# Moving sums, squares and row products in a hybrid decoder layer, and adding the last part's weight blocks on VectorE

## The chip, the cores and the metric

The kernel runs on one core of a Trainium2 chip. The core has five engines with a queue each: TensorE (PE in the profile, its weight loads PEld) multiplies matrices into PSUM banks, VectorE (DVE) and ScalarE (ACT) work on elements, GpSimd (POOL) does small sums and issues transfers that add to what lies at their destination, and SyncE (SP) issues plain transfers. The metric is the device time of one execution in microseconds; of several runs the median counts.

## What is computed

One decoder layer on 512 tokens of width 1024, in float32. Cut to its outline, the reference is:

```python
x = x + 0.5 * swiglu(rms_norm(x, norm_ffn1_w), ffn1_w_in, ffn1_w_out)       # width 2816
x = x + hybrid_mixer(rms_norm(x, norm_mix_w), ...)     # SSD heads beside differential attention
x = x + memory_cross_attention(rms_norm(x, norm_cross_w), rms_norm(mem, norm_mem_w), ...)
x = x + 0.5 * swiglu(rms_norm(x, norm_ffn2_w), ffn2_w_in, ffn2_w_out)
return rms_norm(x, norm_final_w)
```

with

```python
def swiglu(h, w_in, w_out):
    gate, up = jnp.split(h @ w_in, 2, axis=-1)
    return (jax.nn.silu(gate) * up) @ w_out
```

The mixer's SSD half has 16 heads in four groups; each group's output is divided by the root mean square of its 256 columns. The attention half has 8 heads; both halves share an output projection.

## The kernel before

**Products in float32.** TensorE multiplies a rounded format (R32), so each operand is split: ScalarE writes the rounded value (`wh`, line 155) and VectorE the rest (`wl`, line 156), by `split_into`. A product is then three matmuls: high by high, high by low, low by high. Weights pass through a pool: six buffers `wr` for what a transfer brings, three `wh` and three `wl` for the split.

**Two by two blocks.** The big products of both FFNs are done with seven block products instead of eight. For that, sums of weight blocks are needed. Written with the four blocks B11, B12, B21, B22 of a weight, the output projection `out_blocks` uses B11, T1 = B12 + B11, T2 = T1 + B22, B21, B12 + B22, B22 and T4 = T2 + B21, each with its own combination of activation blocks (S1 to S4 and plain ones). Its products run in this order, each as 128x512 matmuls at line 1295: B11 and T1 turn by turn into `oa` and `oe`, T2 with S2 into `ob`, B21 into `oa`, B12 + B22 with S3 into `ob`, B22 with S4 into `oe`, T4 into `ob`. Between them, `oa` is copied into `ob` on ScalarE (line 1362), and `update` (line 1306) adds a finished bank to the running activations `x` on VectorE.

**Where the block sums come from.** In the second FFN they are made ahead of time in device memory (`isum`, `wsum`, by `block_sums_in_dram`). In the first FFN they are made on the way (`here` is true): T1 and B12 + B22 by a transfer from GpSimd that adds the second block to a buffer holding the first (`added`, line 1315), T2 by VectorE out of T1 and a fetched B22 (`t2`, line 1325), in the buffer of T1. T4 needs B21 added to the same buffer. In the first two parts, the fetched B21 is kept (`b21`, `later`) and added by VectorE after the B21 product (line 1372). In the last part `by_dma` is true: B21 is released after its split, and two adding transfers from GpSimd (`t4`, line 1336) read it again during the S3 product.

**Parts.** The 22 tiles of the FFN's inner width come in parts of 6, 8 and 8 (`THIRDS`); `out_blocks` runs once after each, and works on a part's weights in pieces of two tile pairs: in the second and third part, two pieces of 128x1024 a block. In the last part, the load of the memory tiles (`memory_in`) and a table (`prepare`) run beside it.

**Order.** `Order` traces the program. `dense` work is a list of generators that emit TensorE products; `chains` are small generators that yield a number of microseconds, after which they go on. Time in `Order` is the sum of the ideal times of the matmuls emitted. A dense generator that yields a function is blocked until that function is true. For SyncE's and GpSimd's queues the traced order is the order on the engine; on the other engines a planner orders the instructions when the program is built, by the traced order as priority and by when it expects their operands. `behind(ins)` holds what is traced in it behind the given instructions on their engine.

**Row products.** A column of 512 scale factors becomes a row, spread over 128 partitions, by `row_of`: two diagonal matrices (the rounded factors and the rest, line 376) are multiplied by ones into one bank `nrow`, two matmuls one behind the other. In `group` (the SSD groups) both diagonals are made on GpSimd.

**First output tile.** `out_attn` adds the attention half to `x`, four heads a call, eight output tiles. `load_w` fetches and splits a tile's weight. With `prep` all are loaded before the wait for the heads, else each in its turn.

**Squares.** Before the second FFN, `turn_last` transposes the last four tiles of `x`, and `row_of_last` squares them on ScalarE (line 556), 4.0 us later and 2.0 us apart. The first block product of that FFN (`quad` with `fresh`) is in flight then, with its copy of `qa` into `qb` at line 287.

Of the kernel before, what the change touches and what calls it, by code (L numbers as in the profile page):

```python
# [17 lines left out]
P = 128  # L18
# [9 lines left out]
THIRDS = ((0, 6), (6, 8), (14, 8))  # L28
# [9 lines left out]
W = {"h0": 3.4, "hs": 3.3, "ht": 2.0, "hv": 2.08, "hp": 6.75}  # L38
# [62 lines left out]
def body(tc, a, dbg=None):  # L101
# [13 lines left out]
    def nm(s):  # L115
        uid[0] += 1
        return f"{s}_{uid[0]}"

    def s2(s, dt=F32, shape=(P, T)):
        if math.prod(shape[1:]) <= T // 2:  # L120
            return sp.tile(list(shape), dt, tag="s1", name=nm(s), bufs=NHALF)
        return sp.tile(list(shape), dt, tag="s2", name=nm(s))

    def s4(s):
        return sp.tile([P, 4, T // 2], F32, tag=s, name=nm(s), bufs=1)

    def small(s, n, bufs=None):
        return tiny.tile([P, n], F32, tag=s, name=nm(s), bufs=bufs)
# [4 lines left out]
    def aux(s, shape=(P, T)):  # L133
        return aux_p.tile(list(shape), F32, tag="aux", name=nm(s))
# [5 lines left out]
    last, start, last_sum, recent, newest, newest_mm = [], [], [], [], [], []  # L140
    V, S, G = nc.vector, nc.scalar, nc.gpsimd
    od = Order()

    def mm(out, w, x, start, stop):
        od.t += (1 if w.dtype == R32 else 4) * (x.free_size() + 8) / 2400
        newest_mm[:] = [nc.tensor.matmul(out, w, x, start=start, stop=stop).ins]  # L146
# [5 lines left out]
    def split_into(hi, lo, src, scale=None):  # L152
        if scale is None:
            return (
                S.activation(hi, src, AF.Copy),  # L155
                V.tensor_tensor(lo, src, hi.bitcast(F32), ALU.subtract),  # L156
            )
        return (
            S.activation(hi, src, AF.Copy, scale=scale),
            V.scalar_tensor_tensor(lo, src, scale, hi.bitcast(F32), ALU.mult, ALU.subtract),  # L160
        )
# [10 lines left out]
    def load_w(src, n=D):  # L172
        raw = wp.tile([P, n], F32, tag="wr", name=nm("wr"), bufs=6)
        nc.sync.dma_start(raw, src)
        hi = wp.tile([P, n], R32, tag="wh", name=nm("wh"))
        lo = wp.tile([P, n], R32, tag="wl", name=nm("wl"))
        with ExitStack() as after:
            for i in start:
                after.enter_context(tc.issue_after(i))
            recent[:] = [i.ins for i in split_into(hi, lo, raw)]  # L180
        return hi, lo

    @contextmanager
    def behind(ins):
        with ExitStack() as after:
            for i in ins:
                after.enter_context(tc.issue_after(i))
            yield

    H = T // 2  # L190
    S1, S2, S3, S4 = "S1", "S2", "S3", "S4"
# [173 lines left out]
        G.tensor_tensor(col, v, mhalf[:, :nb], ALU.pow)  # L365
        return col

    def row_of(col, nb, first, second, apart):
        ch = tiny.tile([P, nb], R32, tag="ch", name=nm("ch"))
        first.tensor_copy(ch, col)  # L370
        cl = small("cl", nb)
        first.tensor_tensor(cl, col, ch.bitcast(F32), ALU.subtract)
        diags = []
        for eng, c in ((first, ch.bitcast(F32)), (second, cl)):
            diags.append(s2("ndiag", R32, (P, nb, P)))
            eng.tensor_tensor(diags[-1], ident[:, None, :].to_broadcast([P, nb, P]), c[:, :, None].to_broadcast([P, nb, P]), ALU.mult)
        yield apart
        pr = aux("nrow", (P, nb * P))
        with behind(list(newest_mm)):
            for j in range(2):  # L380
                mm(pr, ones_r, diags[j].rearrange("p a b -> p (a b)"), j == 0, j == 1)
        return pr

    class Stat:
# [109 lines left out]
    def ffn1(h, wa, at_out, each, done):  # L494
        xs = []
        wq, plain = iter(a["f1q"]), a["f1i"]
        col4, ncol4 = small("col4", 4, bufs=1), small("ncol4", 4, bufs=1)

        for ti, (_, nf) in enumerate(THIRDS):
            g = []  # L500
            nq = nf // 2
            made = block_tiles(g, nq, True)
            out = out_blocks(a[f"f1b{ti}"], None, g, col4, ncol4, each if ti == len(THIRDS) - 1 else None, n=nq, by_dma=ti == len(THIRDS) - 1)
            if ti == 0:
                th, f = s4("th"), 0
                for ps in ffn_first(h, wa):
                    if ps is None:
                        yield
                    else:
                        gated(*ps, st1.row, th, f)  # L510
                        f += 1
                made(th)
                V.tensor_scalar(col4, st1.col, 0.5, None, ALU.mult)
                V.tensor_scalar(ncol4, st1.col, -0.5, None, ALU.mult)
                for n in range(NPLAIN - 2):
                    for i in ((0, 1), (2,), (3,), ())[n]:
                        blocks = of_halves(h[2 * i], h[2 * i + 1])
                        b11 = tuple(s2("h11" + p_, R32, (P, H)) for p_ in "hl")
                        with behind(start):
                            for to, of in zip(b11, blocks["11"]):  # L520
                                S.activation(to, of.bitcast(F32), AF.Copy)
                        xs.append(block_sums(2 * i, C_FFN1, blocks | {"11": b11}, xf))
                    if n == 3:
                        xf.clear()
                    pg, pu = acc("pg"), acc("pu")
                    yield from proj(pg, load_w(plain[n][0]), h)
                    yield from proj(pu, load_w(plain[n][1]), h)
                    if n % 2 == 0:
                        th = s4("th")
                    if n == NPLAIN - 3:  # L530
                        next(out)
                    gated(pg, pu, st1.row, th, n % 2)
                    if n % 2:
                        made(th)
                h.clear()
                nq -= NPLAIN // 2
            yield from ffn_quads(xs, wq, st1, nq, made, BY_BLOCK, prime=out)
            at_out(ti)
            if ti == len(THIRDS) - 1:
                xs.clear()  # L540
            yield from out
        done()
        banks = [acc, aux, acc, aux]
        yield from turn(1, banks)
        yield from turn(0, banks)
# [303 lines left out]
    wcv = []  # L849

    def out_attn(hg, o0, o1, prep=False):
        ws = {o: load_w(a["woa"][hg, o], 4 * P) for o in range(o0, o1) if prep}
        yield lambda: all(y is not None for y in ya[4 * hg : 4 * hg + 4])
        heads = ya[4 * hg : 4 * hg + 4]
        for o in range(o0, o1):
            po = acc("pm")
            yield from proj(po, ws.get(o) or load_w(a["woa"][hg, o], 4 * P), heads)
            V.tensor_tensor(x[o], x[o], po, ALU.add)
            if prep and len(wcv) < 2:
                wcv.append(load_w(a["wcv"][len(wcv)]))  # L860
        if o1 == KT:
            ya[4 * hg : 4 * hg + 4] = [None] * 4
# [44 lines left out]
    def group(g, bt, ct, xs, zs):  # L907
# [97 lines left out]

        rh = inv_rms_cols(pn, 4, 4.0 / (4 * 256), 4.0 * EPS)
        yield W["gn"]
        pr = yield from row_of(rh, 4, G, G, W["gr"])
        for j in range(2):
            n = 2 * g + j  # L1010
            V.scalar_tensor_tensor(yz[j], yz[j], par[:, C_SSD + n : C_SSD + n + 1], pr, ALU.mult, ALU.mult)
# [252 lines left out]
    def out_blocks(blocks, sums, g, col4, ncol4, each=None, finale=None, clean=True, n=None, by_dma=False):  # L1264

        early = n is not None
        n = n or len(g)
        parts = [(k, min(k + 2, n)) for k in range(0, n, 2)]
# [29 lines left out]
        def product(ps, of, which, first=False, ready=None):  # L1298
            for part in parts:
                w = ready if ready and part == parts[0] else weights(of, part)  # L1300
                for t in range(2):
                    yield from some(ps[t], w, which, part, t, first)
# [36 lines left out]
        here = sums is None  # L1339
        if here:  # L1340
            sums = [t1, added(blocks[B12], blocks[B22], "gate"), t2, lambda part: t_raw[part]]
# [7 lines left out]
        b_ps = [bank[t]("ob") for t in range(2)]  # L1349
# [8 lines left out]
        for m in both:  # L1358
            yield from m
        u2 = []  # L1360
        for t in range(2):
            S.activation(b_ps[t], a_ps[t], AF.Copy)
        for t in range(2):
            update(t + 2, 1, e_ps[t], 1, False)
        yield from product(b_ps, sums[2], S2)
        for t in range(2):
            u2.append(s2("u2"))
            S.activation(u2[t], b_ps[t], AF.Copy)
# [94 lines left out]

    def turn_last():
        yield from turn(1)
        od.spawn(row_of_last(), 4.0)

    def row_of_last():
        for k in range(4, KT):
            with behind(list(newest)):  # L1470
                squared(k, x[k])
            yield 2.0
        yield from row_from(st_2, 3.0)

    od.add(turn_last())
# [90 lines left out]
```

## Time and profile before

| | us |
|---|---|
| runs | 1309.28, 1312.72, 1312.79 |
| median of the runs | 1312.72 |
| the profiled execution, its own time | 1310.71 |
| its span in the profile | 1308.9 |

| engine | busy us | share of the span |
|---|---|---|
| PE | 1288.9 | 98% |
| DVE | 971.9 | 74% |
| ACT | 706.5 | 54% |
| POOL | 119.5 | 9% |

The span runs from the first to the last instruction of the program. Timeline rows have the start in us from there, the duration, engine, line of the kernel, operation, `out<-in` by tile names, shapes and a count; a bracket at the end tells how long the engine sat idle before and what released it. Rows of the same kind that follow each other are merged into one with a count. Rows of waits have who waited for whom, then the total in us, the times and the longest. Matmuls overlap, so the step from one start to the next, and not the duration, is what a matmul costs.

### The profile page before, as it was taken

Reading aid. Unit: us, or ns where it says so; the run is one execution under the profiler, and the core shown is the slowest. Engines: PE = TensorE matmul, PEld = TensorE weight load, DVE = VectorE, ACT = ScalarE, POOL = GpSimd, SP = SyncE. Lnnn points to the kernel's source line nnn. Section 1 sums busy time; section 2 is a strip of 40 time slices with the busy share of each in tenths; the row PEclk is TensorE's granted clock in tenths of the full one; section 3 lists DMA queues with packets and bytes.
Section 4 is the critical chain, followed back from the end, with each engine's and each line's share of the span. In section 5 each row is a group of like instructions: output and inputs, shape, how many; then the busy total and the mean of one; then the engine's idle time right before and its main releaser. Section 6 shows DMA issues by size and latency. Waiting matters only on the chain.

```text
span 1308.9 us, 20080 instructions
## 1 busy us (share of the span) xinstructions
PE 1288.9 (98%) x7709; PEld 1123.8 (86%) x7709; DVE 971.9 (74%) x1542; ACT 706.5 (54%) x1208; POOL 119.5 (9%) x149
## 2 busy tenths in 40 slices
PE   9999999999999999999999999999999999999997
PEld 7879988997887778777788878888889999989995
DVE  6977888787875676567867687645677878877886
ACT  7545564565754564346645465434365646555564
POOL 0001010001110011101012021020001000000000
PEclk9999999999999999999999999999999999999999
DMA  9367777777974525663475638684248876666662
GB/s 339 88 174 187 196 198 196 217 201 203 292 239 146 137 65 148 226 165 105 94 202 156 193 124 240 192 215 131 65 122 249 212 234 179 188 194 180 182 204 96
DMA packets 69263, 234.75 MB, mean 179 GB/s; under 512 B 8160, under 2 KB 9664, under 8 KB 68816
## 3 DMA queue, kind: packets, MB, share of 16 engines
q1 hardware_dynamic: 53200, 180.91, 41.5%
q0 software_dynamic: 13168, 45.67, 19.5%
q10 hardware_dynamic: 2800, 6.91, 1.6%
q8 instruction: 60, 0.98, 0.3%
q14 instruction: 35, 0.29, 0.1%
HBM read 231.30 MB, written 48.29 MB: 214 GB/s over the span
## 4 chain that ended last, share of the span: by engine, by line
PE 75%; issue 13%; DVE 4%; DMA 3%; ACT 2%; POOL 1%; POOLq 0%; SPq 0%; ACTq 0%; DVEq 0%
PE qb L243 11%; PE pm L146 10%; PE qa L243 8%; PE qe L243 7%; PE ob L1295 5%; PE pxbc L146 4%; PE pcq L146 3%; PE pz L146 3%; PE oa L1295 3%; PE oe L1295 3%; DMA wr<-in_f1b 2%; PE pa L146 2%; PE pcv L146 2%; PE pg L146 2%; PE pu L146 2%
## 5 line engine op out<-in xcount | busy, mean ns | idle before, releaser
L155 ACT ACTIVATE wh<-wr 128x1024 fp32r<-128x1024 f32 (+1 forms) x323 | 328.3, 1018 | 339.8 <-issue 60.4
L156 DVE TENSOR_TENSOR wl<-wr,wh 128x1024 fp32r<-128x1024 f32 (+1 forms) x323 | 378.1, 1175 | 138.6 <-ACT wh L155 135.9
L772 ACT ACTIVATE ec<-ec,mn 128x512 f32<-128x512 f32 (+3 forms) x64 | 35.3, 554 | 33.7 <-DVE mn L771 33.7
L146 PE MATMUL pxbc<-hnh,wh 128*128 128x512 f32 x128 | 52.6, 411 | 0.0
L146 PE MATMUL pxbc<-hnh,wl 128*128 128x512 f32 x128 | 50.2, 392 | 0.0
L146 PE MATMUL pxbc<-hnl,wh 128*128 128x512 f32 x128 | 50.2, 392 | 0.0
L243 PE MATMUL qb<-s24h,wh 128*128 128x256 f32 x152 | 43.1, 284 | 0.8 <-ACT qb L287 0.8
L243 PE MATMUL qa<-hmh,wl 128*128 128x256 f32 x152 | 43.1, 284 | 0.1
L243 PE MATMUL qe<-s24h,wl 128*128 128x256 f32 x152 | 43.1, 284 | 0.0
L243 PE MATMUL qa<-h11h,wh 128*128 128x256 f32 x152 | 43.1, 283 | 0.0
L243 PE MATMUL qb<-s24h,wl 128*128 128x256 f32 x152 | 43.0, 283 | 0.0
L243 PE MATMUL qa<-h11h,wl 128*128 128x256 f32 x152 | 43.0, 283 | 0.0
L243 PE MATMUL qb<-s31h,wh 128*128 128x256 f32 x152 | 43.0, 283 | 0.0
L243 PE MATMUL qb<-s31l,wh 128*128 128x256 f32 x152 | 43.0, 283 | 0.0
L243 PE MATMUL qb<-s31h,wl 128*128 128x256 f32 x152 | 43.0, 283 | 0.0
L243 PE MATMUL qa<-hml,wh 128*128 128x256 f32 x152 | 43.0, 283 | 0.0
L243 PE MATMUL qe<-s24h,wh 128*128 128x256 f32 x152 | 43.0, 283 | 0.0
L243 PE MATMUL qa<-h11l,wh 128*128 128x256 f32 x152 | 43.0, 283 | 0.0
L243 PE MATMUL qa<-hmh,wh 128*128 128x256 f32 x152 | 43.0, 283 | 0.0
L243 PE MATMUL qe<-s24l,wh 128*128 128x256 f32 x152 | 43.0, 283 | 0.0
L243 PE MATMUL qb<-hml,wh 128*128 128x256 f32 x152 | 43.0, 283 | 0.0
L243 PE MATMUL qb<-hmh,wh 128*128 128x256 f32 x152 | 43.0, 283 | 0.0
(457 smaller groups left out, 4170.1 us busy)
## 6 DMA issues: line engine op xcount, KB each, us to landing
wr<-in_f2q SPq DMA_DIRECT2D x44, 512.0 KB, 4.5
wr<-in_f1q SPq DMA_DIRECT2D x40, 512.0 KB, 4.5
wr<-in_f1b SPq DMA_DIRECT2D x25, 512.0 KB, 6.6
isum<-in_f2q SPq DMA_DIRECT2D x22, 512.0 KB, 5.2
wr<-isum SPq DMA_DIRECT2D x22, 512.0 KB, 4.1
wsum<-in_f2b SPq DMA_DIRECT2D x20, 512.0 KB, 5.6
wr<-wsum SPq DMA_DIRECT2D x20, 512.0 KB, 4.7
wr<-in_f1q POOLq DMA_DIRECT2D x16, 512.0 KB, 6.8
```

The costliest lines, as they stand in the source:

```text
L146: newest_mm[:] = [nc.tensor.matmul(out, w, x, start=start, stop=stop).ins]
L155: S.activation(hi, src, AF.Copy),
L156: V.tensor_tensor(lo, src, hi.bitcast(F32), ALU.subtract),
L243: newest_mm[:] = [nc.tensor.matmul(out, a_[:, wc], b_, start=first and f == 0 and kp == 0 and j == 0, stop=kp == n - 1 and j == 2, skip_gr ...
L772: S.activation(ec[:, :n], ec[:, :n], AF.Exp, bias=mn, scale=-1.0, accum_out=sm[c][:, i : i + 1])
L1295: newest_mm[:] = [nc.tensor.matmul(ps, a_[:, ts], b_[:, ws], start=first and k == 0 and j == 0, stop=k == n - 1 and j == 2, skip_group_che ...
```

## The change

Five edits. `row_of` gets a parameter `between`: what a chain yields between the two row products; the SSD groups pass 1.2 us, all others nothing. The call of `out_blocks` in the first FFN no longer passes `by_dma`, so the last part too keeps B21 and adds it on VectorE. `out_attn` loads the weight of output tile 0 before it asks for the heads. In `out_blocks`, all sums T2 are traced before the copies and updates ahead of the S2 product, rather than piece by piece within it; only the first FFN does this. `row_of_last` starts at 6.5 us with 1.2 us between squares.

```diff
-    def row_of(col, nb, first, second, apart):
+    def row_of(col, nb, first, second, apart, between=()):
...
-        with behind(list(newest_mm)):
-            for j in range(2):
+        for j in range(2):
+            with behind(list(newest_mm)):
                 mm(pr, ones_r, diags[j].rearrange("p a b -> p (a b)"), j == 0, j == 1)
+            if j == 0:
+                yield from between
         return pr
...
-            out = out_blocks(a[f"f1b{ti}"], None, g, col4, ncol4, each if ti == len(THIRDS) - 1 else None, n=nq, by_dma=ti == len(THIRDS) - 1)
+            out = out_blocks(a[f"f1b{ti}"], None, g, col4, ncol4, each if ti == len(THIRDS) - 1 else None, n=nq)
...
-        ws = {o: load_w(a["woa"][hg, o], 4 * P) for o in range(o0, o1) if prep}
+        ws = {o: load_w(a["woa"][hg, o], 4 * P) for o in range(o0, o1) if prep or o == 0}
         yield lambda: all(y is not None for y in ya[4 * hg : 4 * hg + 4])
...
-        pr = yield from row_of(rh, 4, G, G, W["gr"])
+        pr = yield from row_of(rh, 4, G, G, W["gr"], (1.2,))
...
         u2 = []
+        second = {part: t2(part) for part in parts} if here else {}
         for t in range(2):
             S.activation(b_ps[t], a_ps[t], AF.Copy)
         for t in range(2):
             update(t + 2, 1, e_ps[t], 1, False)
-        yield from product(b_ps, sums[2], S2)
+        yield from product(b_ps, second.get if here else sums[2], S2)
...
-        od.spawn(row_of_last(), 4.0)
+        od.spawn(row_of_last(), 6.5)
...
                 squared(k, x[k])
-            yield 2.0
+            yield 1.2
         yield from row_from(st_2, 3.0)
```

## The prediction

> **What bounds the kernel now.** I read the page first, for the share of each engine.
>
> ```profile
> span 1308.9 us, 20080 instructions
> ...
> PE 1288.9 (98%) x7709; PEld 1123.8 (86%) x7709; DVE 971.9 (74%) x1542; ACT 706.5 (54%) x1208; POOL 119.5 (9%) x149
> ```
>
> TensorE is busy nearly all the time, and no matmul is added or removed. The edit can therefore win only what TensorE now waits for, and lose only by new waits. So I read the waits of TensorE next (total us, times, longest).
>
> ```profile
> PE ob L1295 <- DVE wl L156: 1.7, 3, 0.8
> ...
> PE ob L1295 <- ACT wh L155: 1.1, 1, 1.1
> ...
> PE qb L243 <- ACT qb L287: 0.8, 1, 0.8
> ...
> PE nrow L146 <- POOL ndiag L376: 0.5, 1, 0.5
> ```
>
> These rows are small: 4.1 us together, 0.31% of the span. Then I found each of them in the timelines. The largest cluster is in the last part of the first FFN's output projection, in its product S2 and then in S3:
>
> ```profile
> 316.41 0.39 PE L1295 MATMUL ob<-wh,s24h 128*128 128x512 f32 x1
> ...
> 317.44 0.50 PE L1295 MATMUL ob<-wl,s24h 128*128 128x512 f32 x1 [0.41 <-DVE wl L156]
> ...
> 321.12 0.50 PE L1295 MATMUL ob<-wh,s24h 128*128 128x512 f32 x1 [1.11 <-ACT wh L155]
> ...
> 324.35 0.39 PE L1295 MATMUL oa<-wh,gh 128*128 128x512 f32 x1
> ...
> 332.90 0.40 PE L1295 MATMUL ob<-wh,s31l 128*128 128x512 f32 x1
> 333.82 0.50 PE L1295 MATMUL ob<-wl,s31h 128*128 128x512 f32 x1 [0.53 <-DVE wl L156]
> ```
>
> What S2 takes without waits is shown by the same 24 matmuls of the part before, a piece of the chain of waits:
>
> ```profile
> 195.73 5.44 PE ob L1295 x24
> ```
>
> That is 0.23 us from one to the next. Here S2 takes 324.35 - 316.41 = 7.94 us, so 2.5 are lost. In S3 the step from 332.90 to 333.82 is 0.92 instead of 0.23: 0.7 lost.
>
> **The change, part by part.**
>
> *Sums of the S2 weight pieces made earlier.* VectorE's and ScalarE's rows around it:
>
> ```profile
> 313.17 1.22 DVE L1325 TENSOR_TENSOR wr<-wr,wr 128x1024 f32<-128x1024 f32 x1
> ...
> 314.90 0.75 DVE L1306 SCALAR_TENSOR_TENSOR x<-oe,col,x 128x512 f32<-128x512 f32 x1
> ...
> 316.17 1.23 DVE L156 TENSOR_TENSOR wl<-wr,wh 128x1024 fp32r<-128x1024 f32 x1
> ...
> 318.75 1.23 DVE L1325 TENSOR_TENSOR wr<-wr,wr 128x1024 f32<-128x1024 f32 x1
> 321.10 1.22 DVE L156 TENSOR_TENSOR wl<-wr,wh 128x1024 fp32r<-128x1024 f32 x1 [1.12 <-ACT wh L155]
> ```
> ```profile
> 320.01 1.06 ACT L155 ACTIVATE wh<-wr 128x1024 fp32r<-128x1024 f32 x1 [3.14 <-DVE wr L1325]
> ```
>
> The second sum runs at 318.75, behind two running-sum updates (L1306) of which one is shown; ScalarE's split waits 3.14 us for it, TensorE 1.11 us for the split. Now both sums stand ahead of the copies and updates, so the second can run after the first. No sum is added here, one of 1.23 us is moved ahead, and what is queued behind it is the low split of the first piece (316.17), which already ended (317.40) too late for TensorE. In the bad order that split is 1.2 us later: the 0.4 us wait grows to 1.6 and S2 wins only 2.5 - 1.6 = 0.9, with the second split then in time. In the good order (the sum in a hole of VectorE before 316) it wins 2.5. In the part before, S2 has nothing to win (its 5.44 above), and the third wait of ob on wl (0.8 of the 1.7 us) lies in S3 of the first part, whose sums stay: I take 0 for both. SyncE's fetches keep their order, five of this projection one after another with nothing of another line between them, so no queue is passed:
>
> ```profile
> 298.59 16.15 SPq L1276 DMA_DIRECT2D wr<-in_f1b  x5
> ...
> 320.00 0.33 SPq L1276 DMA_DIRECT2D wr<-in_f1b  x1
> 323.88 5.96 SPq L174 DMA_DIRECT2D wr<-in_wck  x3
> ```
>
> The fetch at 320.00 leaves when the second sum (318.75 + 1.23 = 319.98) gives its buffer back, so it will leave 2 to 4 us sooner.
>
> *The last running sums by VectorE.* Two adding transfers on GpSimd's queue (L1336) go; block 21, fetched anyway, stays in its two buffers and is added by two more VectorE sums (2 x 1.22 = 2.44 us) after the 12 product's splits. Is there room? Busy us in two stretches: PE, PEld, DVE, ACT, POOL; then clock, DMA share and GB/s.
>
> ```profile
> 316.00:324.40 8.40, 6.82 (x28) 4.64 (x27) 7.28 (x10) 4.83 (x8) 2.54 (x5) 1.00 0.94 242
> 324.40:336.00 11.60, 11.07 (x48) 8.62 (x47) 8.33 (x13) 6.89 (x14) 1.70 (x3) 1.00 1.05 276
> ```
> ```profile
> 324.90 0.69 DVE L1369 TENSOR_TENSOR oe<-oe,u 128x512 f32<-128x512 f32 x1
> 328.26 1.22 DVE L156 TENSOR_TENSOR wl<-wr,wh 128x1024 fp32r<-128x1024 f32 x1 [2.66 <-ACT wh L155]
> ...
> 332.54 1.23 DVE L156 TENSOR_TENSOR wl<-gate,wh 128x1024 fp32r<-128x1024 f32 x1 [0.61 <-ACT wh L155]
> ```
>
> VectorE is free for 11.60 - 8.33 = 3.27 us of the second stretch, 2.66 of them in one hole ending at 328.26. The sums fit into that hole: cost 0; without it, up to 2.44. They hold the buffers longer: the wck fetches of 323.88, next in SyncE's queue, wait for them until 324.90 + 0.69 + 1.22 = 326.8 and 328. Their first user starts far behind:
>
> ```profile
> 350.54 0.48 PE L146 MATMUL pck<-hm,wh 128*128 128x256 f32 x2
> ```
>
> So this costs nothing. What S3 waits for is something else, the landing of its own two adding transfers:
>
> ```profile
> 327.17 1.06 ACT L155 ACTIVATE wh<-wr 128x1024 fp32r<-128x1024 f32 x1 [2.94 <-DMA wr<-in_f1b]
> ...
> 331.45 1.06 ACT L155 ACTIVATE wh<-gate 128x1024 fp32r<-128x1024 f32 x1 [1.55 <-DMA gate<-in_f1b]
> ```
>
> The second piece lands at 331.4, its low split ends at 332.54 + 1.23 = 333.77, and TensorE uses it at 333.82: no slack. If that landing stays, everything that S2 wins is waited for again in S3, and the two edits together win 0. If it comes earlier by d, they win d, at most 2.5 + 0.7 = 3.2. The DMA engines are full there (share 0.94 and 1.05), and the change takes two adding transfers of 512 KB and for some 3 us two fetches out of that stretch. Bounds 0 and 3.2; I take 1.4, just under the middle, since the first piece (327.17) leaves S3 only some 0.9 us of room by itself: its low split ends at 328.26 + 1.22 = 329.48, and its first use is 11 matmuls ahead of the one at 332.90, at about 330.4.
>
> *The row products of the SSD groups* are parted by 1.2 us of other matmuls.
>
> ```profile
> 780.42 0.49 PE L146 MATMUL nrow<-ndiag,ones_r 128*128 128x512 f32 x1
> 781.42 0.49 PE L146 MATMUL nrow<-ndiag,ones_r 128*128 128x512 f32 x1 [0.50 <-POOL ndiag L376]
> ...
> 815.67 0.62 PE L146 MATMUL nrow<-ndiag,ones_r 128*128 128x512 f32 x2
> ```
> ```profile
> 780.34 1.03 POOL L376 TENSOR_TENSOR ndiag<-ident,cl 128x512 fp32r<-128x512 f32 x1
> ```
>
> In group 2 the second product comes 1.00 us after the first instead of 0.23, since GpSimd's diagonal ends at 781.37. With 1.2 us between it is ready: 0.77 won. In the last group the two run together (815.67). There the order is blocked until the group is done, so no matmul falls between them: 0; were it held back, the first output projection would wait up to 1.2. The group's scaling comes 1.2 us later elsewhere, long before its use. I take 0.8 won.
>
> *The first output tile's load* is traced before the wait for the heads, not after.
>
> ```profile
> 502.29 0.60 PE L150 MATMUL pot<-ident,on 128*128 128x128 f32 x4
> ...
> 511.04 0.40 PE L146 MATMUL pm<-yah,wh 128*128 128x512 f32 x1
> ```
>
> The last head's transposes (502.29) precede the first output matmul (511.04) by 8.7 us and it shows no wait: the condition holds when it is asked, and nothing moves. 0.
>
> *The squares before the second FFN* start 2.5 us later and stand closer.
>
> ```profile
> 976.07 1.06 ACT L155 ACTIVATE wh<-wr 128x1024 fp32r<-128x1024 f32 x1 [0.25 <-PE qa L243]
> 977.03 0.58 ACT L287 ACTIVATE qb<-qa 128x512 f32<-128x512 f32 x1
> ```
>
> The copy that TensorE waits 0.8 us for stands behind a weight split, and that split had waited 0.25 us for TensorE, with ScalarE idle: the square ahead of it was done by then. Moving the square frees nothing unless it also changes who goes first. Bounds 0 and 0.8; I take 0.3, a third of it.
>
> **Sum.** 1.4 + 0.8 + 0.3 = 2.5 us. The profiled run took 1310.71 us (span 1308.9 and 1.8 around it), so 1308.2 against it; the runs' median, 1312.72, lies 2.0 higher, so 1310.2.
>
> **Rivals.**
> - *All of it comes back.* S2 2.5, S3 0.7, the row product 0.8, the copy 0.8: 4.8, so 1307.9. For it: each edit stands at a place with a wait. Against: it needs the S3 transfers over 3 us sooner.
> - *The adding transfers were hidden anyway.* They were issued after those S3 needs. Landing times of the two removed, then of all twelve that stay in the first FFN (min, median, max):
>
> ```profile
> DMA to landing us min/median/max: 11.9/13.5/15.2
> ...
> DMA to landing us min/median/max: 4.3/8.1/9.6
> ```
>
>  The removed ones took 13.5 us against 8.1, as if they stood behind the others rather than beside them. Then S3's landings stay, part three wins 0, and only 0.8 + 0.3 is left: 1311.6. [...]
> - *VectorE becomes the bound of part three (slower).* The moved sum delays the first low split by 1.2 and the two new sums stand ahead of S3's splits instead of in the hole: 1.2 + 2.44 = 3.7 and nothing won, 1316.4, more if the wck fetches wait as well. It decides when the new sums start after 327. For it: VectorE is busy 7.28 of 8.40 us in S2. Against: the hole of 2.66 us, right behind the splits that the sums follow.
>
> **How the numbers follow.** Forecast 1310.2 (its own range 1308.9 to 1311.6): 0.40. All back: 0.22. Hidden anyway: 0.13. Slower: 0.25. A change under 0.3% (3.9 us, the spread of the three runs) can't be told from none. Faster than 1308.8 is the second case and a quarter of the first: 0.32. Slower than 1316.7 is two thirds of the last: 0.17. The rest, 0.51, is the same. The range 1307.0 to 1315.8 leaves out the edge of the second case and part of the last.
>
> **What would show it.** Right: the wait on ACT wh near 321 gone, both L1325 sums together near 314, two L1372 sums before 329, the gate piece's split starting near 330, no nrow wait on POOL. Wrong: L1372 behind L1306 at 331; the S3 wait grown to 2 us with the same landing (hidden anyway); a wait at pck; new waits of 1 us in the SSD groups, whose hand order shifts by 1.2 us.

## The result and the profile after

| | us |
|---|---|
| before, median of 7 runs beside the change | 1310.82 (1308.98 to 1312.79) |
| after, median of 7 runs | 1316.65 (1314.33 to 1317.26) |
| ratio, with its 95% interval | 1.0038 [1.0025, 1.005] |
| the profiled execution after, its own time and span | 1317.26 and 1315.5 |

The change makes the kernel 0.38% slower, 5.8 us. The forecast was 2.5 us faster (1310.2, reckoned from 1312.72, the median of the first three runs). In the code of after the lines stand 2 or 3 lower: L1295 is now L1297, L1325 is L1327, L1372 is L1375, L1011 is L1013.

TensorE's waits after (who waited for whom; total us, times, longest), the rows that answer to those of before:

```profile
PE ob L1297 <- DVE wl L156: 4.7, 3, 2.1
PE pq L146 <- DVE vl L156: 3.1, 1, 3.1
...
PE qb L243 <- ACT qb L287: 0.8, 1, 0.8
...
PE nrow L146 <- POOL ndiag L376: 0.5, 1, 0.5
```

The second row is new. The wait of `ob` on `wh` (1.1) is gone, and that on `wl` has grown from 1.7 to 4.7. The waits that the row products and the squares were to end, `nrow` and `qb`, are what they were. The two stretches that lost most follow.

**SSD group 0, near 560 us.** The profiled execution after is 2.08 us behind that of before at the first row product (560.59 against 558.51), 5.09 us at the first matmul of `pq` (567.71 against 562.62) and 6.68 us at the 14th (572.38 against 565.70): 4.6 us are lost here. TensorE's timeline after, and then before:

```profile
560.59 0.39 PE L146 MATMUL nrow<-ndiag,ones_r 128*128 128x512 f32 x1
...
562.20 0.39 PE L146 MATMUL nrow<-ndiag,ones_r 128*128 128x512 f32 x1
...
567.71 0.50 PE L146 MATMUL pq<-hnh,wh 128*128 128x512 f32 x1 [3.06 <-DVE vl L156]
...
568.98 0.63 PE L146 MATMUL pq<-hnh,wl 128*128 128x512 f32 x1
...
572.38 0.39 PE L146 MATMUL pq<-hnl,wh 128*128 128x512 f32 x1
```
```profile
558.51 0.62 PE L146 MATMUL nrow<-ndiag,ones_r 128*128 128x512 f32 x2
...
562.62 0.50 PE L146 MATMUL pq<-hnh,wh 128*128 128x512 f32 x1
...
565.70 0.39 PE L146 MATMUL pq<-hnl,wh 128*128 128x512 f32 x1
```

The second row product comes 1.61 us after the first; six matmuls of the value projection `pv` lie between them. The query projection `pq`, which started without a wait before, waits 3.06 us. VectorE after, and before:

```profile
562.63 1.41 DVE L1013 SCALAR_TENSOR_TENSOR y<-y,par,nrow 128x512 f32<-128x512 f32 x2 [1.57 <-PE nrow L146]
564.08 1.35 DVE L156 TENSOR_TENSOR ysl<-y,ysh 128x512 fp32r<-128x512 f32 x2
565.83 1.22 DVE L156 TENSOR_TENSOR wl<-wr,wh 128x1024 fp32r<-128x1024 f32 x1 [0.40 <-ACT wh L155]
566.97 2.48 DVE L156 TENSOR_TENSOR vl<-pv,vh 128x512 fp32r<-128x512 f32 x4
```
```profile
559.17 1.41 DVE L1011 SCALAR_TENSOR_TENSOR y<-y,par,nrow 128x512 f32<-128x512 f32 x2 [0.18 <-PE nrow L146]
560.62 1.35 DVE L156 TENSOR_TENSOR ysl<-y,ysh 128x512 fp32r<-128x512 f32 x2
561.89 1.28 DVE L156 TENSOR_TENSOR vl<-pv,vh 128x512 fp32r<-128x512 f32 x2
563.75 1.23 DVE L156 TENSOR_TENSOR wl<-wr,wh 128x1024 fp32r<-128x1024 f32 x1 [0.58 <-ACT wh L155]
```

ScalarE after:

```profile
563.42 1.29 ACT L155 ACTIVATE ysh<-y 128x512 fp32r<-128x512 f32 x2 [3.61 <-DVE y L1013]
564.74 1.06 ACT L155 ACTIVATE wh<-wr 128x1024 fp32r<-128x1024 f32 x1
...
565.71 2.04 ACT L155 ACTIVATE vh<-pv 128x512 fp32r<-128x512 f32 x4
```

The scaling of `y` waits for the second row product, with VectorE idle for 1.57 us. Behind it stand the two splits of `y`, and behind these the splits of `pv` into `vh` and `vl`. These free the four accumulation banks that `pv` holds, and `pq` needs one of them. Before, the first of the two `vl` of 561.89 (0.68 of the 1.28 us) ended at 562.57, 0.05 us ahead of `pq`. After, a weight split (`wh`, `wl`) that had stood behind the first two `v` splits stands ahead of all four. So `vl` starts at 566.97.

Behind the wait, the matmuls step 0.43 us apart (568.98 to 572.38 are eight steps) instead of 0.23. The stretches after, with the busy us of PE, PEld, DVE, ACT, POOL, then TensorE's granted clock, DMA share and GB/s, and one of before:

```profile
564.00:568.00 4.00, 0.94 (x4) 0.48 (x4) 3.56 (x6) 3.68 (x7) 0.81 (x1) 1.00 0.99 256
568.00:572.00 4.00, 4.00 (x13) 3.09 (x13) 1.45 (x3) 0.00 (x0) 0.00 (x0) 0.62 0.97 303
572.00:576.00 4.00, 4.00 (x18) 3.30 (x17) 0.00 (x0) 1.08 (x2) 0.00 (x0) 0.96 0.04 18
```
```profile
562.00:566.00 4.00, 3.94 (x18) 2.95 (x17) 3.42 (x5) 2.25 (x4) 0.81 (x1) 1.00 0.91 245
```

The granted clock falls to 0.62 in the 4 us from 568 on, and read finer it is 0.97 from 568 to 569, 0.50 from 569 to 572 and 0.82 from 572 to 573. Eight steps, 0.2 us longer each, are 1.6 us; with the 3.0 us by which `pq` starts later, they make the 4.6 us.

**The last part of the first FFN.** TensorE in S2, and at S3:

```profile
317.54 0.40 PE L1297 MATMUL ob<-wh,s24h 128*128 128x512 f32 x1
...
320.76 0.50 PE L1297 MATMUL ob<-wl,s24h 128*128 128x512 f32 x1 [2.14 <-DVE wl L156]
...
325.43 0.39 PE L1297 MATMUL oa<-wh,gh 128*128 128x512 f32 x1
...
333.17 0.50 PE L1297 MATMUL ob<-wl,s31h 128*128 128x512 f32 x1 [1.69 <-DVE wl L156]
```

S2 takes 325.43 - 317.54 = 7.89 us, where it took 7.94. Its waits of 0.41 and 1.11 have become one of 2.14; with S3's they have grown by 1.8 us (2.14 + 1.69 - 0.41 - 1.11 - 0.53). VectorE, ScalarE and GpSimd:

```profile
314.30 1.22 DVE L1327 TENSOR_TENSOR wr<-wr,wr 128x1024 f32<-128x1024 f32 x1
...
316.04 1.22 DVE L1327 TENSOR_TENSOR wr<-wr,wr 128x1024 f32<-128x1024 f32 x1
...
319.49 1.22 DVE L156 TENSOR_TENSOR wl<-wr,wh 128x1024 fp32r<-128x1024 f32 x1
...
325.52 2.35 DVE L1375 TENSOR_TENSOR wr<-wr,wr 128x1024 f32<-128x1024 f32 x2
330.50 0.70 DVE L1372 TENSOR_TENSOR oe<-oe,u 128x512 f32<-128x512 f32 x1 [2.62 <-ACT u L1371]
...
331.89 1.22 DVE L156 TENSOR_TENSOR wl<-wr,wh 128x1024 fp32r<-128x1024 f32 x1
```
```profile
328.92 1.06 ACT L155 ACTIVATE wh<-wr 128x1024 fp32r<-128x1024 f32 x1 [4.05 <-DMA wr<-in_f1b]
...
331.70 1.06 ACT L155 ACTIVATE wh<-gate 128x1024 fp32r<-128x1024 f32 x1
```
```profile
320.75 0.87 POOL L1317 DMA_DIRECT2D wr<-in_f1b  x1 [17.90 <-DVE wl L156]
```

Both T2 sums now stand ahead of the first piece's low split (319.49), which S2 waits for. The two sums that replace the adding transfers run at 325.52, in VectorE's hole. S3's first weight piece lands later than before (its split at 328.92, against 327.17), since GpSimd's issue of it waits until that same low split is done (320.71); from issue to landing it takes 8.1 us, as before (8.2). The second piece's split starts about when it did (331.70, against 331.45).

S3's wait of 1.69 us is for the first piece's low split, and by these rows the order on VectorE makes it (no run tests that alone). ScalarE's split of that piece is done at 329.98 (328.92 + 1.06), but VectorE's starts only at 331.89: it stands behind an update of `oe` (330.50) that waits for ScalarE's copy `u`, which ScalarE makes after its split. Started at 329.98, it would have ended at 331.20 by its 1.22 us, just ahead of its use (due at 331.09 + 0.23, one step behind the matmul before it). Before, it stood ahead of that update, at 328.26:

```profile
329.40 0.69 DVE L1369 TENSOR_TENSOR oe<-oe,u 128x512 f32<-128x512 f32 x1
```

### The profile page after: what moved, and what is told of

Same layout as the page of the kernel before. It is cut to its first block, busy times and chain, and to the rows that moved or that the text cites. A ratio compares the mean times of both kernels' runs of the same rounds, so it can differ in the third digit from the quotient of the medians.

```text
span 1315.5 us, 20076 instructions
## 1 busy us (share of the span) xinstructions
PE 1289.9 (98%) x7709; PEld 1124.6 (85%) x7709; DVE 974.3 (74%) x1544; ACT 707.4 (54%) x1208; POOL 118.6 (9%) x147
## 4 chain that ended last, share of the span: by engine, by line
PE 75%; issue 13%; DMA 4%; DVE 4%; ACT 2%; POOL 1%; POOLq 0%; SPq 0%; ACTq 0%; DVEq 0%
PE qb L243 11%; PE pm L146 10%; PE qa L243 7%; PE qe L243 7%; PE ob L1297 5%; PE pxbc L146 4%; PE oa L1297 3%; PE pcq L146 3%; PE oe L1297 3%; PE pz L146 3%; DMA wr<-in_f1b 2%; PE pa L146 2%; PE pcv L146 2%; PE pq L146 2%; PE pg L146 2%
## 5 line engine op out<-in xcount | busy, mean ns | idle before, releaser
L243 PE MATMUL qb<-hmh,wl 128*128 128x256 f32 x152 | 43.0, 283 | 0.0
```

The costliest lines, as they stand in the source:

```text
L243: newest_mm[:] = [nc.tensor.matmul(out, a_[:, wc], b_, start=first and f == 0 and kp == 0 and j == 0, stop=kp == n - 1 and j == 2, skip_gr ...
```

## The experiments

Every ratio is to the kernel before on the same chip, with its 95% interval.

### Which of the edits

All edits but the parted row products:

```diff
-        pr = yield from row_of(rh, 4, G, G, W["gr"], (1.2,))
+        pr = yield from row_of(rh, 4, G, G, W["gr"])
```

> All five edits but the 1.2 us between the row products. Theory: the parted row product of SSD group 0 holds VectorE's queue, so the value splits and with them the banks of the next projection come late (3.06 us of wait, then some 1.6 us of slow clock). Then this kernel shows no wait of pq on vl, full clock there, and takes about 4.8 us less than the changed kernel: some 1312 us against 1310.8 before (ratio about 1.001). Rival: the wait at pq comes from the shift of the work ahead (part three of the first FFN is 1.7 us later). Then it stays and the time is about 1316.5 (1.004).

Measured: 1311.34 us, ratio 1.0007 [0.9994, 1.0019]; no wait at `pq`. In the last part of the first FFN its profiled execution waits 1.67 and 1.01 us where after shows 2.14 and 1.69.

The parted row products alone, with `between` of `row_of` and the call above as in the change, and nothing else:

> The kernel before with the 1.2 us between the row products alone. Theory: the wait of pq on vl of about 3 us and the slow clock behind it are there, time about 1315.6 (ratio 1.0037). Rival (they come from the sums ahead): no such wait, time as before, 1310.8. In both the wait of nrow on GpSimd in group 2 stays at 0.5 us, since its two products stay adjacent in the order.

Measured: 1316.03 us, ratio 1.0046 [1.0028, 1.0063]. The wait of 3.06 us stands at `pq`, with slow steps behind it (0.42 to 0.43 us from 565.42 on, a granted clock of 0.66 from 566 to 570); the wait of 0.50 us in group 2 is still there. So this edit alone makes the whole slowdown, and the other four together nothing that can be told from none.

### Which group

The parting in group 0 alone, then in all others:

```diff
-        pr = yield from row_of(rh, 4, G, G, W["gr"])
+        pr = yield from row_of(rh, 4, G, G, W["gr"], (1.2,) if g == 0 else ())
```
```diff
-        pr = yield from row_of(rh, 4, G, G, W["gr"])
+        pr = yield from row_of(rh, 4, G, G, W["gr"], (1.2,) if g else ())
```

> The kernel before with the two row products parted by 1.2 us in the first SSD group alone. Theory (the slowdown is made in the first group: the scaling comes some 1.4 us late, the weight's split then goes ahead of two splits of v, the q projection waits 3.1 us and its next eight products run at half clock): about 1315.9, the whole of what the parting in all groups showed (1316.0 against 1310.8 in those runs), with the wait of 3.1 us and the slow steps in the trace. Rival (the groups behind it bring part of it): 1312 to 1314.

> The kernel before with the products parted by 1.2 us in the second, third and last group, adjacent in the first. Theory: 1310.8, no change; the 0.5 us wait of the third group stays, since the planner sets six products ahead of the first row product there instead of between the two. Rival: 1312 to 1314, with a wait in one of these groups that was not there.

Measured: 1314.17 us, 1.0038 [1.0022, 1.0054], for group 0; 1310.82 us, 1.001 [1.0, 1.0019], for the others (before: 1309.85). Group 0 carries 4.3 us; the 1.0 us of the others is at the edge of its interval, and its trace shows no wait in these groups that was not there before. The expectation of 1315.9 for group 0 lies inside its interval, so how much the other groups bring is open. In group 2 no other product stands between the row products: TensorE's order there is that of before, with the same 1.00 us from the first to the second. Probably the planner expects GpSimd's diagonal late and fills the time in front of the first. So there the edit neither helps nor harms.

### How group 0 loses it

Three `pv` matmuls between the row products instead of six:

```diff
-        pr = yield from row_of(rh, 4, G, G, W["gr"])
+        pr = yield from row_of(rh, 4, G, G, W["gr"], (0.3,) if g == 0 else ())
```

> The kernel before with the products of the first group parted by 0.3 us instead of 1.2: three products of v stand between them, not six, and the weight's split passes one split of v instead of two. Theory (lateness counts, from the first tenth: the q projection begins in the very 0.06 us in which its bank comes free): a wait of 0.7 to 0.8 us ahead of the first q product, no slow steps, since the wait is short; 1311.5. Rival (any parting sets off the clock, or the whole 3 us): over 1314. Rival (the planner had slack): 1310.8 and no wait.

Measured: 1312.07 us, 1.0016 [1.0005, 1.0026]. TensorE's row:

```profile
564.78 0.50 PE L146 MATMUL pq<-hnh,wh 128*128 128x512 f32 x1 [0.73 <-DVE vl L156]
```

The wait is what three matmuls take (3 x 0.23 = 0.69). There was no slack at all, and the steps behind the wait stay at 0.23 us. The time rose by 2.2 us, more than the 0.7 of the wait; the interval begins at 0.65 us and allows it.

Both row products side by side, but planned 1.2 us later:

```diff
-        pr = yield from row_of(rh, 4, G, G, W["gr"])
+        pr = yield from row_of(rh, 4, G, G, W["gr"] + (1.2 if g == 0 else 0.0))
```

> The kernel before with the two products of the first group side by side, but both planned 1.2 us later, so both stand behind the six products of v that the change put between them. The instruction order of ScalarE and VectorE is the same as with the parting. Theory (it is the second product's lateness, not the parting, that costs): as with the parting, about 1315.9, wait of 3.1 us and slow steps. Rival (parting itself, the bank held open or the planner's waiting list, costs): 1310.8 to 1312.

Measured: 1315.66 us, 1.0045 [1.003, 1.0059]. TensorE's timeline, and then its stretch behind the wait (columns as above):

```profile
560.52 0.62 PE L146 MATMUL nrow<-ndiag,ones_r 128*128 128x512 f32 x2
...
566.28 0.50 PE L146 MATMUL pq<-hnh,wh 128*128 128x512 f32 x1 [3.06 <-DVE vl L156]
```
```profile
566.00:570.00 4.00, 3.72 (x16) 3.09 (x17) 2.02 (x4) 0.31 (x1) 0.00 (x0) 1.00 1.11 309
```

Unparted, the same wait and about the same time: it is the lateness of the second product that costs, not the parting. One part of the expectation failed. In this profiled execution the clock stayed at 1.00 behind the same 3.06 us. It took 1314.56 us, 1.1 less than the median of its runs; its mean granted clock was 0.997, that of its other four runs 0.996.

Last, the parting in group 0, with the weight split that passed the `v` splits held behind all four of them (it belongs to the query projection of head 5, two projections ahead):

```diff
         vs[hg] = [split("v", pv[tb]) for tb in range(4)]
+        v_last[:] = last
...
-        yield from proj(pq, load_w(a["wq"][hd]), h)
+        with behind(v_last if hd == 5 else []):
+            wq = load_w(a["wq"][hd])
+        yield from proj(pq, wq, h)
```

> The products parted by 1.2 us in the first group alone, and the weight's split that then passed v's splits held behind all four of them; everything else stands as with the parting alone. Theory (the wait of 3.1 us is 1.4 us of lateness, six products of v, and 1.7 us of the weight's two splits ahead of v's, and only the long wait halves the clock): a wait of 1.3 to 1.5 us ahead of the first q product, no slow steps; 1.3 to 1.9 us over the kernel before, 1312.2 to 1312.9. Rival (the weight's split only moved where it did no harm, the lateness alone makes the wait): 3.1 us and slow steps as before, 4.3 to 5.8 us over the kernel before.

Measured: 1312.48 us, 1.0012 [1.0001, 1.0024] (before: 1310.62).

```profile
564.09 0.50 PE L146 MATMUL pq<-hnh,wh 128*128 128x512 f32 x1 [1.43 <-DVE vl L156]
```

The wait falls from 3.06 to 1.43 us, which is the lateness of six matmuls (6 x 0.23 = 1.38), and no slow steps follow (0.23 us each). The mean granted clock of its twelve runs was 0.997 or 0.998, that of the parting in group 0 alone 0.996 or 0.997. So the 3.06 is 1.4 of lateness and 1.6 of the weight split that the planner put ahead of the late `v` splits; the clock comes on top (0.81 from 562 to 566 and 0.76 from 566 to 570 in the parting in group 0 alone).

### The last part of the first FFN

The T2 sums made early, alone:

```diff
         u2 = []
+        second = {part: t2(part) for part in parts} if here else {}
...
-        yield from product(b_ps, sums[2], S2)
+        yield from product(b_ps, second.get if here else sums[2], S2)
```

> The kernel before with the T2 sums ahead of the copies and updates alone; the last part keeps its adding transfers. Theory: the second sum goes ahead of the first low split, which comes 2 us later; S2 waits 2.1 us once instead of 0.4 + 1.1, S3 then waits about 1.5 us longer: 1 to 2 us slower, 1312 to 1313 (1.001). Rival (the two new sums of block 21 cost the time): no change, 1310.8.

Measured: 1310.89 us, 1.0001 [0.9989, 1.0013] (before: 1310.77). The wait for the second sum is gone, and S2 waits 2.13 us for the first low split instead. The loss of 1 to 2 us that was expected did not show.

The last part's running sums on VectorE, alone:

```diff
-            out = out_blocks(a[f"f1b{ti}"], None, g, col4, ncol4, each if ti == len(THIRDS) - 1 else None, n=nq, by_dma=ti == len(THIRDS) - 1)
+            out = out_blocks(a[f"f1b{ti}"], None, g, col4, ncol4, each if ti == len(THIRDS) - 1 else None, n=nq)
```

> The kernel before with block 21 added on VectorE in the last part alone. Theory: the two sums fall into VectorE's hole near 326, S2 keeps its waits of 0.4 and 1.1 us, the S3 wait is 0 to 0.5 us: time as before or 0.5 us less, 1310.3 to 1310.8 (0.9996 to 1.000). Rival (the new sums cost the time): S3 waits 1 us more, 1312 (1.001).

Measured: 1314.66 us, 1.0032 [1.0018, 1.0045]; a loss that no theory had. VectorE, GpSimd and TensorE in S2:

```profile
320.31 1.22 DVE L1372 TENSOR_TENSOR wr<-wr,wr 128x1024 f32<-128x1024 f32 x1
323.62 0.17 DVE L370 CAST ch<-ncol 128x2 fp32r<-128x2 f32 x1 [2.09 <-POOL ncol L365]
323.69 1.22 DVE L156 TENSOR_TENSOR wl<-wr,wh 128x1024 fp32r<-128x1024 f32 x1
```
```profile
321.98 0.87 POOL L1315 DMA_DIRECT2D gate<-in_f1b  x1 [1.33 <-ACT hm L159]
322.54 1.04 POOL L365 TENSOR_TENSOR ncol<-nv,mhalf 128x2 f32<-128x2 f32 x1
```
```profile
324.96 0.79 PE L1295 MATMUL ob<-wl,s24h 128*128 128x512 f32 x1 [2.25 <-DVE wl L156]
```

The cast that reads the memory's inverse root (`ncol`) stands on VectorE ahead of S2's second low split, probably because the planner expects the root sooner with the two transfers gone from GpSimd's queue. But the root stands behind the gate piece's transfer there, and that transfer's issue had waited 1.33 us itself. VectorE sits idle for 2.09 us on a cast of 128x2, with the split that TensorE needs right behind it. The clock then falls to 0.61 (columns as above):

```profile
324.00:328.00 4.00, 3.04 (x7) 2.46 (x8) 3.87 (x5) 0.60 (x1) 0.00 (x0) 0.61 1.05 242
```

To test this, the cast goes to GpSimd, behind the root:

```diff
-            pr = yield from row_of(self.col, nb, V, V, rows)
+            pr = yield from row_of(self.col, nb, V if nb > 2 else G, V, rows)
```

> The kernel before with block 21 completed by VectorE's sums, and the small cast of the memory's inverse root (2 columns) moved from VectorE to GpSimd, where it stands right behind the root that it reads. Theory (alone, this edit cost 3.9 us because that cast stood on VectorE ahead of a low split and waited 2.1 us for GpSimd, whose root stood behind the gate piece's transfer issue, and the wait of TensorE that came of it halved the clock): without the cast there no wait of 2.25 us and no slow steps; 1310.8 to 1311.8. Rival (the sums themselves are too much for VectorE): 1313.5 or more, as with the cast.

Measured: 1312.2 us, 1.0009 [0.9995, 1.0022] (before: 1311.29). The 2.25 us wait is gone, and the loss is down to a size that can't be told from none. So that small cast made the wait, and probably most of the loss. That is not shown in full: the two intervals overlap, the ten runs spread from 1307.8 to 1316.26 us, and the profiled execution, at 1313.56, has a new wait in S3 with slow steps behind it (0.43 us from 333.84 on, a granted clock of 0.70 from 332 to 336):

```profile
332.92 0.50 PE L1295 MATMUL ob<-wl,s31h 128*128 128x512 f32 x1 [1.80 <-DVE wl L156]
```

It is the one that after has there: VectorE's low split (331.65) stands behind the update that waits for ScalarE (330.25). With the cast in place this order is the same, but TensorE comes to S3 too late to wait for it. In the whole change the early T2 sums shift the planner's order, and the cast isn't placed there.

### A version that beats both?

If the second T2 sum costs what it stands in front of on VectorE, GpSimd could make it. Once on the kernel before, once on the change without the parting, both with the early T2 sums:

```diff
-            V.tensor_tensor(t_raw[part], t_raw[part], more, ALU.add)
+            (G if here and each is not None and part[0] else V).tensor_tensor(t_raw[part], t_raw[part], more, ALU.add)
```

> The kernel before with both T2 sums made early in each part, as the change does, and the second one of part three on GpSimd instead of VectorE; the adding transfers stay. GpSimd needs about 2.1 us for it by twice its 128x512 row (1.03 us) and stands idle there. Theory (the early second sum costs what it stands in front of on VectorE, the low split of the first piece): the wait ahead of S2's third product falls from 2.1 us to under 0.9, no wait on the second piece's sum; 1309.3 to 1310.0, 0.8 to 1.5 us under the kernel before. Rival (GpSimd's sum is late or slows VectorE's splits): 1310.8 or more, with S2's wait on the second piece back.

> The change without the parting of the row products, and with the second T2 sum of part three on GpSimd. VectorE places one of block 21's sums ahead of the second piece's low split instead. Theory (moving the stall, not removing it): S2's first wait under 0.9 us, but a wait of about 1 us on the second piece's low split; 1310.3 to 1311.0. Rival (all waits of S2 gone): 1309.3 to 1310.0.

Measured: 1311.23 us, 1.0003 [0.9995, 1.0012], and 1312.12 us, 1.0008 [0.9999, 1.0017]. No gain. GpSimd, VectorE and TensorE of the first of the two:

```profile
311.95 2.46 POOL L1325 TENSOR_TENSOR wr<-wr,wr 128x1024 f32<-128x1024 f32 x1 [10.73 <-DVE wl L156]
```
```profile
312.12 2.85 DVE L156 TENSOR_TENSOR s31l<-s,s31h 128x512 fp32r<-128x512 f32 x1
```
```profile
315.02 0.50 PE L1295 MATMUL oe<-wh,s31l 128*128 128x512 f32 x1 [2.33 <-DVE s31l L156]
```

VectorE's split of `s31l` began 0.17 us after GpSimd's sum and took 2.85 us; in after the same split takes 0.68. TensorE waited 2.33 us for it. S2's own wait was gone, as expected, but the one that came for it, one product earlier, is as long. The second of the two waits 2.36 us in the same place and 2.03 us more ahead of S4. Nothing tried here beats the kernel before.

## Why the prediction was wrong

**The step that failed** is a sentence on the row products: "The group's scaling comes 1.2 us later elsewhere, long before its use." The use of the scaled `y` is indeed far off. But on VectorE and ScalarE the splits of `v`, which TensorE needs at once, stood behind the scaling and its two splits, and none went ahead of them: in after, the first bank of `pv` has, by the kernel's order, its last matmul at 559.68, and ScalarE still sits idle for 3.61 us, until 563.42, for the scaled `y`. The first of the splits ended 0.05 us ahead of `pq` before. The sum had +0.8 us for this edit; in group 0 alone it lost 4.3. The loss is 1.4 of lateness, 1.6 of the planner's new order, and the clock's fall (0.50 from 569 to 572 us in after), which the prediction had no term for. The trace of before showed the first of the three: nobody had to know more than what was queued behind L1011. The prediction did name "new waits of 1 us in the SSD groups" as a sign against itself, but gave them no chance and no price.

**Group 2's 0.77 us** was not won. The prediction took it that the filling matmuls fall between the two products; in the built program no product stands between the two.

**Part three's 1.4 us** was not won: the four other edits together come to 1.0007 [0.9994, 1.0019]. The order that the prediction called bad is the one that came: the first low split stands behind both sums. It priced that at a wait of 1.6 us and 0.9 won; the split also fell behind the two updates, the wait was 2.14, and S2 won nothing. For S3 it took the landing of the second weight piece as the bound, between no sooner and 3.2 us sooner. In after that piece's split starts no sooner. In the change without the parting it starts at 329.71, 1.7 us sooner than before, and S3 still waits 1.01 us: for the first piece's low split, behind the update that VectorE now does first. The prediction had no term for that order. No gain from the removed transfers shows in the landings: from issue to landing the two pieces take 8.1 and 9.1 us after, 8.2 and 8.6 before, as the rival *The adding transfers were hidden anyway* had it. That the new sums fit in VectorE's hole (325.52, "before 329") was right. That the edit alone costs 3.9 us was foreseen nowhere.

**The squares'** 0.3 us was 0: the wait of 0.8 stayed. The reason that the prediction gave against its own number, a weight split ahead of the copy, held. **The first output tile** at 0 was right: its load does not move.

**The slower rival** gave 1316.4 us, near the 1316.65 that came, but that is luck. Its first half happened, the late low split in S2; its second did not, since VectorE held the two sums in its hole. The four edits without the parting cost nothing that can be told from none; the time was lost in SSD group 0.

## What to carry to other kernels

Before an instruction is moved later, list what stands behind it on every engine that it feeds, and how much slack the first of those has that TensorE waits for; that the result's own use is far away says nothing. Where a planner orders engines by expected times, a small shift can change which work goes first elsewhere, so price an edit together with the reordering that it sets off. A small instruction that waits for another engine can hold up a needed split behind it: here a cast of 0.17 us, with VectorE idle for 2.09 us ahead of it, and 2.25 us of wait on TensorE.

## What the hardware showed that was not expected

**The clock falls behind waits of 1.8 to 3.1 us, but not always.** TensorE's longest waits in the profiled executions, and the granted clock in the windows of 4 us behind them (in brackets the windows, in us):

| kernel, place | wait us | clock behind |
|---|---|---|
| after, `pq` | 3.06 | 0.62, 0.96 (568 to 576) |
| parted products alone | 3.06 | 0.91, 0.66 (562 to 570) |
| parted in group 0 alone | 3.06 | 0.81, 0.76 (562 to 570) |
| both products later, `pq` | 3.06 | 1.00, 1.00 (566 to 574) |
| second T2 sum on GpSimd, on the change without the parting | 2.36; 2.03 | 1.00 (316 to 320); 1.00 (332 to 336) |
| second T2 sum on GpSimd, on the kernel before | 2.33 | 0.58, 0.57 (316 to 324) |
| running sums on VectorE alone, S2 | 2.25 | 0.61, 0.96 (324 to 332) |
| after, S2; early T2 sums alone, S2 | 2.14; 2.13 | 1.00, 1.00 (320 to 328); the same |
| running sums on VectorE, cast on GpSimd, S3 | 1.80 | 0.70 (332 to 336) |
| after, S3; the change without the parting, S2 | 1.69; 1.67 | 1.00 (332 to 336); steps of 0.23 us |
| weight split behind `v`, `pq` | 1.43 | steps of 0.23 us |

An estimate of how long the slow spells are: at 0.50, which is what the clock behind `pq` in after reads from 569 to 572, a spell lasts twice what the granted clock lacks. That gives (0.38 + 0.04) x 4 x 2 = 3.4 us there, the same for the parted products alone, for those parted in group 0 alone and for the running sums on VectorE alone (0.43 x 4 x 2 each), and (0.42 + 0.43) x 4 x 2 = 6.8 us, twice that, in the longest.

That longest one, with the second T2 sum on GpSimd (columns as above):

```profile
316.00:320.00 4.00, 4.00 (x11) 1.98 (x11) 3.85 (x7) 2.49 (x5) 0.88 (x1) 0.58 0.89 291
320.00:324.00 4.00, 4.00 (x12) 3.14 (x11) 3.54 (x5) 2.40 (x3) 3.05 (x4) 0.57 0.98 250
```

Equal waits end differently: behind 3.06 us the clock fell to 0.62 in after, and stayed at 1.00 with both products later. Nor does the longer wait decide: 1.80 us came with 0.70, 2.36 with 1.00. What decides was not settled; other work ahead of each wait differs too.

**A GpSimd sum held up VectorE.** A VectorE subtraction (`s31l`) that takes 0.68 us in after took 2.85 beside a GpSimd sum of 2.46 and ended 0.56 us after it (at 314.97 against 314.41), much as if it had begun there. On the change without the parting, too, it took 2.84 us beside a sum of 2.46. Before has such a place too: of VectorE's eight rows of line 949 (128x256, median 0.42 us) the longest, 1.30 us at 780.35, ran beside GpSimd's `ndiag` of 1.03 us at 780.34. What makes it, no run here tests, nor whether VectorE holds up GpSimd in the same way.
